# A hybrid decoder step: the scan's buffers in three pools, its skip connection at the group's end, attention spread over 15 blocks

## The chip, the core and the metric

The kernel runs on one core of one Trainium2 chip. A core has five engines that work side by side: TensorE (PE, matrix products; its weight loads are listed as PEld), VectorE (DVE), ScalarE (ACT), GpSimd (POOL) and SyncE (SP, which here only issues transfers). Sixteen DMA engines move data between DRAM and the on-chip memory SBUF. PE writes its results to PSUM, from where DVE and ACT fetch them. The metric is the device time of one execution in microseconds (us); lower is better.

## What is computed

One layer of a decoder, for a prompt of 1024 tokens and eight sample sequences of one token each, all in float32. Three branches read the same normalised input through one input projection, and their results are weighted by gates, added, projected, and followed by a gated feed-forward part. Cut to what matters here:

```
sc_b, sc_c, sc_x, z, xbc, dt_raw, q, gates = split(xn @ w_in)
y_a = (sc_b * conv3(sc_c * sc_x)) @ w_sc_out
xs, bm, cm = split(silu(conv4(xbc) + bias));  dt = softplus(dt_raw + dt_bias)
# scan over chunks of 128 tokens; 4 groups of 8 heads x 64, state 128
y_diag[i] = sum_j (c_i . b_j) * exp(acum_i - acum_j) * dt_j * x_j      (j <= i, same chunk)
y_off[i]  = exp(acum_i) * (c_i . state)
state     = chunk_decay * state + sum_j b_j * decay_j * dt_j * x_j
y_ssd = (y_diag + y_off + ssm_d * xs) * silu(z)
y_b = group_rmsnorm(y_ssd) @ w_ssm_out
y_c = softmax(q @ mem_k.T / 16) @ mem_v @ w_attn_o                      (256 memory tokens, 4 heads)
x += (g_A*y_a + g_B*y_b + g_C*y_c) @ w_merge_o;  x += swiglu(rmsnorm(x));  rmsnorm(x)
```

The term `ssm_d * xs` is called the skip below. The eight sample tokens take the same path with a state of their own; in the kernel they are columns 1024 to 1031 of tiles that are 1032 wide.

## The kernel before

Activations are kept transposed: 128 features on the partitions, 1032 tokens along the row. A float32 product is made of three products of rounded operands (high by high, high by low, low by high). One output block of 128 features is 8 input tiles x 3 products x 3 column thirds of 344, that is 72 matmuls, in `gemm` (the matmuls have line L203). Its weights come from DRAM and are split into a high and a low half by ACT and DVE (L152, L153).

The stretch in question runs as follows. First come the last gate products (`gate_pair`, L775 to L779 write their outputs to `gt_d`). Then 20 blocks of the list `fillers` and of the first output product (eight q blocks `ps_q`, four gate blocks `ps_g`, and the eight blocks `wo00` to `wo07`) run while the scan is worked off in pieces. Then attention is worked off in pieces while the second and third output products run (`wo10` to `wo17`, `wo20` to `wo27`). Then the attention output product `wo30` to `wo37` and the merge follow.

The mixing is done by a queue `pend` of small functions. `gemm` calls `tick()` several times among its matmuls, and each tick runs one function of the queue. `pace` holds how many ticks a block gets and the fraction carried over. This gives the order in the program. A scheduler then sets the order of each engine's instructions, with program order as priority, by its own estimate of when operands are ready; on the chip each engine keeps that order.

The scan, `ssd_pieces`, goes through four groups of eight chunks each, and a chunk is made in three pieces. `first` transposes b and x, makes the masked product `cbm`, multiplies it into the decay matrix `r` and makes `xdt` and `xdd`. `second` makes the state's part `po` and the chunk's part `py` (L941), adds them in `yt` (L937, L946) and adds the skip into x, one operation for each of four feature tiles (L950). `third` updates the state `s`. The decay matrix starts as a broadcast load of `ac_d` into `r` (L882), and ACT makes it ready (`prep`, L888, L889). `s_skip` (L990) does the skip of the eight sample columns. `final` writes out the state. Then `z_pieces` multiplies by silu(z) (L1039) and sums squares (L1047), and `group_norm` makes the sums on PE (`psny`, L1060), spreads the result, scales and stores to `yb_d` (L1084, L1087).

SBUF is divided into pools that open and close like a stack on either side. The scan's tiles are all in one pool, `ssd`, on the right side. It is opened after the pool of the operand forms (`xfx`, 24768 bytes a partition at the outer end) and that of the gate and convolution outputs (`pxa`, next to it) have closed, and lies over parts of both. A group of five shared buffers (`ev`, each 1036 wide) serves most short-lived full-width tiles, and each is taken again once it is free.

Attention ends with the sample's outputs: `s_out` for each of eight sequences, four pieces that write out convolution states (`conv_state`), and `s_back`, which transposes the sample outputs (`psob`, L1509) and stores them to `at_d` (L1511). `out_ahead` and `out_in` load `at_d` (L1301) and split it into the eight inputs `b00` to `b07` of `wo30` (L162, L163).

Of the kernel before, what the change touches and what calls it, by code (L numbers as in the profile page):

```python
# [9 lines left out]
F32 = mybir.dt.float32  # L10
F32R = mybir.dt.float32r
AF = mybir.ActivationFunctionType
ALU = mybir.AluOpType
# [4 lines left out]
P = 128  # L18
D = 1024
T = 1024  # L20
NS = 8
TT = T + NS
# [4 lines left out]
KD = D // P  # L27
EPS = 1e-6
LAG = 3
GROUPS = 4  # L30
HEADS = 32
HPG = 8
# [9 lines left out]
def tile_kernel(ctx: ExitStack, tc, a, o):  # L42
    nc = tc.nc
    V, S, G, PE, SY = nc.vector, nc.scalar, nc.gpsimd, nc.tensor, nc.sync
# [4 lines left out]
    def bc(ap, shape):  # L49
        return ap.to_broadcast(shape)  # L50
# [13 lines left out]
    def sm_ps(name):  # L64
        return psm.tile([P, 512], F32, tag="sm", name=name)
# [4 lines left out]
    def act_tile(part, name, dt=F32R, shape=(P, TT)):  # L70
        return ap_.tile(list(shape), dt, tag=part, name=name)
# [84 lines left out]
    def ev_tile(name, shape=(P, TT + 4), dt=F32):  # L156
        return ev.tile(list(shape), dt, tag="ev", name=name)
# [8 lines left out]
    pend = deque()  # L166
# [12 lines left out]
    pace = [3, 0.0]  # L179
# [209 lines left out]

    ph1 = ExitStack()  # L390
    cn = ph1.enter_context(tc.tile_pool(name="cn", bufs=1))
    h_sc = cn.tile([P, 8, 16], F32, tag="h_sc", name="h_sc")
    h_xc = cn.tile([P, 24, 24], F32, tag="h_xc", name="h_xc")
    xn = [(act_tile("ah", f"xnh{k}"), act_tile("al", f"xnl{k}")) for k in range(KD)]
    xw = [act_tile(("ah", "al")[k % 2], f"xw{k}", F32) for k in range(KD)]
    ps_dt, ps_b0 = mm_ps("ps_dt"), mm_ps("ps_B0")
# [1 line left out]
    with tc.tile_pool(name="p0", bufs=1) as p0:  # L398
# [12 lines left out]
        at = 0  # L411
        for key, src, n in (
# [11 lines left out]
            r = flat_src.rearrange("(r c) -> r c", c=P)  # L424
# [76 lines left out]
        for g3 in range(3):  # L501
            c, n_all = span(g3)
# [17 lines left out]
    for src, dst, nr, nt in (  # L520
# [4 lines left out]
        for q0 in range(0, nt, per):  # L525
            t = ev_tile(f"hist{nr}_{q0}", (nr, per * P))
# [10 lines left out]
    dtT = cn.tile([P, 9, HEADS], F32, tag="dtT", name="dtT")  # L537
    decst = cn.tile([P, NCK, HEADS], F32, tag="decst", name="decst")
    cdec = cn.tile([P, NCK, HEADS], F32, tag="cdec", name="cdec")
    dts = cn.tile([P, 16, NS], F32, tag="dts", name="dts")  # L540
    es = cn.tile([P, 16, NS], F32, tag="es", name="es")
    dpar = cn.tile([P, 16], F32, tag="dpar", name="dpar")
    ys = cn.tile([P, 16, NS], F32, tag="ys", name="ys")
    bcs = cn.tile([P, GROUPS, NS, 2], F32, tag="bcs", name="bcs")

    dt_stack = ExitStack()
    pd_ = dt_stack.enter_context(tc.tile_pool(name="pdt", bufs=1))
# [240 lines left out]
    ssd = ExitStack()  # L788
    pool = {}

    def b3(t, n):
        return t.rearrange("p (a b) -> p a b", a=n)

    def sp_tile(shape, tag, name, bufs=2):
        return pool["ssd"].tile(shape, F32, tag=tag, bufs=bufs, name=name)


    def bc_rows():
# [67 lines left out]
        pair()  # L866
        assert not pend

    def ssd_pieces(g, xg, bcg):
        hs = slice(g * HPG, (g + 1) * HPG)  # L870
        h0 = g * HPG
        state = {}
# [4 lines left out]

        def load(c):
            nm = f"{g}_{c}"
            r = sp_tile([P, HPG, P], "r", "r" + nm, 3)  # L880
            live[c] = r
            SY.dma_start(r, ac_d[g, c].unsqueeze(0).to_broadcast([P, HPG, P]))  # L882

# [7 lines left out]
        def load_ea(c):  # L891
            ea = None
            if c > 0:
                ea = sp_tile([P, 4, P], "ea", f"ea{g}_{c}")
                for k in range(2):
                    SY.dma_start(ea[k * 64 : (k + 1) * 64], ea_d[g, c, 4 * k : 4 * k + 4].unsqueeze(0).to_broadcast([64, 4, P]))
            return ea
# [27 lines left out]
        def second(c):  # L925
            nm = f"{g}_{c}"
            cs = slice(c * P, (c + 1) * P)
            r, ea, xdt, xdd, bT = live[c]
            yt = sp_tile([P, 4, P], "yt", "yt" + nm, 1)
            if c > 0:  # L930
                po = sm_ps("po" + nm)
                for t in range(4):
                    PE.matmul(  # L933
                        po[:, t * P : (t + 1) * P], state["s"][:, t * P : (t + 1) * P], bcg[1][:, cs],
                        start=True, stop=True,
                    )
                V.tensor_tensor(yt, b3(po, 4), ea, op=ALU.mult)  # L937
            py = sm_ps("py" + nm)
            for h in range(HPG):
                hp = (h % 2) * 64  # L940
                PE.matmul(  # L941
                    py[hp : hp + 64, (h // 2) * P : (h // 2 + 1) * P],
                    xdt[:, h * 64 : (h + 1) * 64], r[:, (h % 2) * 4 + h // 2, :], start=True, stop=True,
                )
            if c > 0:
                V.tensor_tensor(yt, b3(py, 4), yt, op=ALU.add)  # L946
            else:
                S.copy(yt, b3(py, 4))
            for t in range(4):
                V.scalar_tensor_tensor(  # L950
                    xg[t][:, cs], xg[t][:, cs], dpar[:, g * 4 + t : g * 4 + t + 1], yt[:, t, :],
                    op0=ALU.mult, op1=ALU.add,
                )

        def third(c):
            nm = f"{g}_{c}"
            r, ea, xdt, xdd, bT = live.pop(c)
            pss = sm_ps("pss" + nm)
            PE.matmul(pss, bT, xdd, start=True, stop=True)  # L959
            if c == 0:  # L960
                s_new = sp_tile([P, 512], "s", "s" + nm)
                ins = V.tensor_copy(s_new, pss)
            else:
                s_new = state["next"]
                ins = V.tensor_tensor(s_new, pss, s_new, op=ALU.add)  # L965
            state["s"] = s_new
            return ins.ins

        def decay(c):

            s_new = sp_tile([P, 512], "s", f"s{g}_{c}")
            G.tensor_tensor(  # L972
                b3(s_new, HPG), b3(state["s"], HPG), bc(cdec[:, c, hs].unsqueeze(2), [P, HPG, 64]),
                op=ALU.mult,
            )
            state["next"] = s_new

        def final():
            ps = sm_ps(f"psf{g}")
            for t in range(4):  # L980
                PE.transpose(ps[:, t * P : (t + 1) * P], state["s"][:, t * P : (t + 1) * P], ident)
            sf = sp_tile([P, 4, P], "yt", f"sf{g}", 1)
            S.copy(sf, b3(ps, 4))
            SY.dma_start(
                o["p_ssm"][0, 0, hs].rearrange("h p n -> (h p) n").rearrange("(t q) n -> q t n", q=P), sf
            )

        def s_skip():
            for t in range(4):
                V.scalar_tensor_tensor(  # L990
                    xg[t][:, T:TT], xg[t][:, T:TT], dpar[:, g * 4 + t : g * 4 + t + 1], ys[:, g * 4 + t, :],
                    op0=ALU.mult, op1=ALU.add,
                )

        def head():
            load(0)
# [34 lines left out]
    def z_load(g, t, hold):  # L1031
        zs = act_tile(("ah", "al")[t % 2], f"zs{g}{t}", F32)
        SY.dma_start(zs, zs_d[g * 4 + t])
        hold[t] = zs

    def z_pieces(g, xg, hold):
        def piece(t):
            zs = hold.pop(t)
            V.tensor_mul(xg[t], xg[t], zs)  # L1039
            if t == 0:  # L1040
                hold["q"] = ev_tile(f"sqa{g}")
            sqa = hold["q"]
            if t == 0:
                S.activation(sqa[:, :TT], xg[t], AF.Square)
            else:
# [236 lines left out]
    gate_pair(18, plain)  # L1282
    st_stack.close()
    pa_stack.close()
    pmm[0] = mm_stack.enter_context(tc.tile_pool(name="pmm1", bufs=2, space=PSUM))


    pool["ssd"] = ssd.enter_context(tc.tile_pool(name="ssd", bufs=2, side="right"))
    fillers = deque()
    for i in range(8):  # L1290
        fillers.extend(q_step(i))
# [61 lines left out]
    outs = deque()  # L1353
# [8 lines left out]
        )  # L1362
    for g in range(GROUPS):
        xg, bcg, hold = groups[g]
        pieces = ssd_pieces(g, xg, bcg)
        if g > 0:
            pend.extend([lambda g=g: load_group(g), None])
        pend.extend(pieces[:-3])
        pend.append(lambda g=g, hold=hold: [z_load(g, t, hold) for t in range(2)])
        pend.extend(pieces[-3:])  # L1370
        pend.extend(z_pieces(g, xg, hold) + [None] + group_norm(g, xg, hold))
    pace[0] = len(pend) / (len(fillers) + KD)
    while fillers or pend:
        if len(fillers) == 1:
            out_ahead(sc_d)
# [24 lines left out]
    at = att_stack.enter_context(tc.tile_pool(name="att", bufs=2))  # L1400
    if True:
# [170 lines left out]
        pieces = [[(kv_in, 0)], [(kv_in, 1), (a_load, 0)], [], []]  # L1572
# [23 lines left out]
        pend.extend(pieces)  # L1596
        pend.extend(states)
        pend.extend([None, s_back])
        pace[0] = 5
        while pend:  # L1600
            run_next(outs)
        pace[0] = 3
        att_stack.close()
        ph2 = ctx.enter_context(tc.tile_pool(name="ph2", bufs=1))
        assert not pend
# [82 lines left out]
    for half in range(2):  # L1688
        sq = ev_tile(f"sq{half}")
        for m in range(KD):  # L1690
# [16 lines left out]
            t = x2[m][:, HS[half]]  # L1707
# [237 lines left out]
```

## Time and profile before

| | before |
|---|---|
| median of 3 runs | 2502.28 us (2502.19 to 2504.86) |
| profiled execution | 2503.04 us, span of its trace 2501.3 us |
| matmuls | 18714 |
| busy: PE, DVE, ACT, POOL | 2461.6, 1519.3, 1047.0, 135.3 us |
| scan with its 20 blocks | about 966 to 1333 us |
| attention with its 14 blocks | about 1333 to 1566 us |
| DMA moved | 392.08 MB, mean 157 GB/s |

A row of the profile gives line, engine, operation, the tiles written and read, their shapes and the count, then busy time, mean duration in ns, and the idle time ahead of the instructions with what ended it. "issue" means that nothing the profile shows was waited for. In a row of the timeline the first number is the start in us from the beginning of the span and the second the time taken.

### The profile page before, as it was taken

To read this page: it belongs to the slowest core of one execution; us is meant where nothing else is said; L and a number is where in the kernel's file an instruction comes from. 1 tells how busy PE (TensorE), PEld (TensorE's weight loads), DVE (VectorE), ACT (ScalarE), POOL (GpSimd) and SP (SyncE) were. 2 spreads that over 40 slices of the span, in tenths; PEclk is the share of its full clock that TensorE was granted. 3 is DMA by queue.
4 is the path that set the end of the run, shared out by engine and by line. 5 is a ranking of instruction groups with operands and counts; after the bars stand their busy time and mean duration, and the time that the engine had idled before them with its cause. 6 is when DMAs were issued, how large, how long until landed. Compare 5 with 4: busy or idle time off the path is not lost.

```text
span 2501.3 us, 44971 instructions
## 1 busy us (share of the span) xinstructions
PE 2461.6 (98%) x18714; PEld 2399.9 (96%) x18714; DVE 1519.3 (61%) x2590; ACT 1047.0 (42%) x1688; POOL 135.3 (5%) x163
## 2 busy tenths in 40 slices
PE   7999999999999999999999999999999999999998
PEld 6999999999999998999989998999999999999998
DVE  6754586777677773766866662655775545453325
ACT  6554455454545534556545441223433333341212
POOL 0300000000000000321120000000000000000000
PEclk9999999999999999999999999999999999999999
DMA  6344434344344455668867686945442222282211
GB/s 202 110 150 154 128 104 143 110 140 126 99 136 136 127 160 190 192 211 266 276 199 277 218 303 218 327 144 178 140 151 95 85 68 85 86 274 89 68 34 69
DMA packets 348331, 392.08 MB, mean 157 GB/s; under 512 B 15334, under 2 KB 285782, under 8 KB 348119
## 3 DMA queue, kind: packets, MB, share of 16 engines
q1 hardware_dynamic: 327678, 331.50, 42.1%
q10 hardware_dynamic: 20449, 57.71, 6.1%
q8 instruction: 147, 2.41, 0.4%
q14 instruction: 57, 0.47, 0.1%
HBM read 280.40 MB, written 108.98 MB: 156 GB/s over the span
## 4 chain that ended last, share of the span: by engine, by line
PE 92%; DVE 2%; DMA 2%; ACT 2%; issue 1%; SPq 0%; ACTq 0%; DVEq 0%; POOL 0%
PE po L203 14%; PE pd L203 9%; PE ps_q L203 4%; PE pm L1701 4%; PE py L941 1%; PE pss L959 1%; PE ps_g L203 1%; PE po L933 1%; PE ps_z L203 1%; PE u20m L248 1%; PE u6m L248 1%; PE g20m L248 1%; PE u18m L248 1%; PE g18m L248 1%; PE u16m L248 1%
## 5 line engine op out<-in xcount | busy, mean ns | idle before, releaser
L1843 DVE TENSOR_TENSOR x<-pd,x 128x1032 f32<-128x1032 f32 x24 | 29.6, 1231 | 131.2 <-PE pd L203 131.2
L888 ACT ACTIVATE r<-r,acum 128x128 f32<-128x128 f32 x256 | 78.8, 391 | 5.3 <-DMA r<-ac_d 4.9
L659 DVE SCALAR_TENSOR_TENSOR ax<-u,prm,ax 128x1024 f32<-128x1024 f32 x44 | 56.3, 1280 | 0.1
L920 POOL TENSOR_TENSOR xdd<-xdt,decst 128x512 f32<-128x512 f32 x32 | 38.0, 1189 | 296.5 <-DVE xdt L916 296.5
L829 ACT ACTIVATE st<-st,es 128x128 f32<-128x128 f32 x128 | 41.9, 394 | 22.4 <-DMA st<-in_state_ssm_dram 20.5
L914 DVE TENSOR_TENSOR r<-r,cbm 128x1024 f32<-128x1024 f32 x32 | 39.0, 1218 | 9.5 <-ACT r L889 9.2
L1348 DVE TENSOR_TENSOR yr<-po,yr 128x1032 f32<-128x1032 f32 x8 | 9.9, 1232 | 53.8 <-PE po L203 53.8
L913 ACT COPY bT<-bp 128x128 f32<-128x128 f32 x32 | 8.5, 265 | 79.9 <-DVE cbm L911 79.9
L831 DVE SCALAR_TENSOR_TENSOR st<-sr,dts,st 128x128 f32<-128x128 f32 x128 | 40.2, 346 | 0.4
L941 PE MATMUL py<-r,xdt 128*64 128x128 f32 x512 | 35.9, 284 | 4.4 <-issue 4.4
L937 DVE TENSOR_TENSOR yt<-po,ea 128x512 f32<-128x512 f32 x28 | 19.3, 689 | 32.5 <-PE po L933 29.7
L941 PEld LDWEIGHTS py<-r,xdt 128*64 128x64 f32 x512 | 28.1, 139 | 8.7 <-issue 5.3
L950 DVE SCALAR_TENSOR_TENSOR x<-x,dpar,yt 128x128 f32<-128x128 f32 x128 | 36.2, 345 | 0.2
L835 DVE SCALAR_TENSOR_TENSOR sr<-st,sr 128x128 f32<-128x128 f32 x128 | 35.4, 286 | 1.1
L972 POOL TENSOR_TENSOR s<-s,cdec 128x512 f32<-128x512 f32 x28 | 35.1, 1253 | 0.5 <-DVE s L965 0.4
L889 ACT ACTIVATE r<-r 128x1024 f32<-128x1024 f32 x32 | 33.9, 1060 | 0.6
L959 PE MATMUL pss<-xdd,bT 128*128 128x512 f32 x64 | 33.5, 605 | 0.0
L1708 DVE TENSOR_TENSOR x<-pm,xT 128x516 f32<-128x516 f32 x16 | 11.1, 696 | 36.4 <-PE pm L1701 36.3
L933 PE MATMUL po<-bc,s 128*128 128x128 f32 x224 | 29.5, 275 | 0.0
L933 PEld LDWEIGHTS po<-bc,s 128*128 128x128 f32 x224 | 28.4, 191 | 0.0
L1630 DVE TENSOR_TENSOR gt<-po,gt 128x1032 f32<-128x1032 f32 x8 | 9.9, 1232 | 30.6 <-PE po L203 28.8
L662 DVE SCALAR_TENSOR_TENSOR ax<-u,prm,ax 128x1032 f32<-128x1032 f32 x22 | 28.3, 1286 | 0.0
(9105 smaller groups left out, 8947.7 us busy)
## 6 DMA issues: line engine op xcount, KB each, us to landing
r<-ac_d SPq DMA_DIRECT2D x32, 512.0 KB
gt<-gt_d SPq DMA_DIRECT2D x24, 516.0 KB
xs_d<-ax ACTq DMA_DIRECT2D x22, 516.0 KB
hr<-h_d SPq DMA_DIRECT2D x22, 516.0 KB
gt_d<-G ACTq DMA_DIRECT2D x20, 516.0 KB
x<-xs_d SPq DMA_DIRECT2D x16, 516.0 KB
zs<-zs_d SPq DMA_DIRECT2D x16, 516.0 KB
yb_d<-x SPq DMA_DIRECT2D x16, 516.0 KB
```

The source lines that it names most:

```text
L203: PE.matmul(ps[:, n, :CW], wt[:, ks], x[:, n * CW : (n + 1) * CW], start=(k == 0 and i == 0), stop=(k == nk - 1 and i == 2),)
L248: PE.matmul(ps[:, n, :HC], wt[:, ks], x[:, n * HC : (n + 1) * HC], start=(start and kt == 0 and i == 0), stop=(kt == 3 and i == 2), skip_g ...
L659: V.scalar_tensor_tensor(acc[:, :T], u[:, j : j + T], w[j], acc[:, :T], op0=ALU.mult, op1=ALU.add)
L829: S.activation(st[:, i], st[:, i], AF.Copy, scale=es[:, g * 4 + i, b : b + 1])
L831: V.scalar_tensor_tensor(st[:, i], rb, dts[:, g * 4 + i, b : b + 1], st[:, i], op0=ALU.mult, op1=ALU.add)
L888: S.activation(r[:, j, :], r[:, j, :], AF.Relu, scale=-1.0, bias=acum[:, c, h : h + 1])
L914: V.tensor_tensor(r, r, bc(cbm.unsqueeze(1), [P, HPG, P]), op=ALU.mult)
L920: G.tensor_tensor(b3(xdd, HPG), b3(xdt, HPG), bc(decst[:, c, hs].unsqueeze(2), [P, HPG, 64]), op=ALU.mult)
L933: PE.matmul(po[:, t * P : (t + 1) * P], state["s"][:, t * P : (t + 1) * P], bcg[1][:, cs], start=True, stop=True,)
L941: PE.matmul(py[hp : hp + 64, (h // 2) * P : (h // 2 + 1) * P], xdt[:, h * 64 : (h + 1) * 64], r[:, (h % 2) * 4 + h // 2, :], start=True, s ...
L959: PE.matmul(pss, bT, xdd, start=True, stop=True)
L1701: PE.matmul(ps[:, n, :HC], wt[:, ks], x[:, half * HT + n * HC : half * HT + (n + 1) * HC], start=(k == 0 and i == 0), stop=(k == KD - 1 an ...
```

## The change

Four things are changed.

- The tiles that only the phase ahead of the scan needs (`h_sc`, `h_xc`, `dts`, `es`, `bcs`) move into a pool `ch` of their own, which is closed ahead of the scan. The scan's single pool becomes three, opened in the order `ssr` (the three `r` buffers), `ssd` (`cbm`, `bT`, `xdt`, `xdd`) and `ssy` (`ea`, `s` and the new `y`).
- The outputs of a group's chunks are written to one tile `y` of 4 x 1032, one buffer, in place of `yt` of 4 x 128. The skip is no longer added chunk by chunk; it is one full-width operation for each feature tile at the head of each piece in `z_pieces`. The sample columns are copied into `y` (four copies in place of sixteen small operations). The state that `final` writes out takes an `ev` buffer in place of `yt`.
- The pace in the scan is set anew with its carried fraction at zero and a millionth added.
- The pace in attention, 5 pieces a block, becomes the number of pieces divided by the blocks that are left but one (15).

```diff
-    h_sc = cn.tile([P, 8, 16], F32, tag="h_sc", name="h_sc")
-    h_xc = cn.tile([P, 24, 24], F32, tag="h_xc", name="h_xc")
+    ch_stack = ExitStack()
+    ch = ch_stack.enter_context(tc.tile_pool(name="ch", bufs=1))
+    h_sc = ch.tile([P, 8, 16], F32, tag="h_sc", name="h_sc")
+    h_xc = ch.tile([P, 24, 24], F32, tag="h_xc", name="h_xc")
...
-    def sp_tile(shape, tag, name, bufs=2):
-        return pool["ssd"].tile(shape, F32, tag=tag, bufs=bufs, name=name)
+    def sp_tile(shape, tag, name, bufs=2, at="ssd"):
+        return pool[at].tile(shape, F32, tag=tag, bufs=bufs, name=name)
...
-            r = sp_tile([P, HPG, P], "r", "r" + nm, 3)
+            r = sp_tile([P, HPG, P], "r", "r" + nm, 3, "ssr")
...
-                ea = sp_tile([P, 4, P], "ea", f"ea{g}_{c}")
+                ea = sp_tile([P, 4, P], "ea", f"ea{g}_{c}", at="ssy")
...
-            yt = sp_tile([P, 4, P], "yt", "yt" + nm, 1)
+            if c == 0:
+                hold["y"] = sp_tile([P, 4, TT], "y", f"y{g}", 1, "ssy")
+            yt = hold["y"][:, :, cs]
...
-            for t in range(4):
-                V.scalar_tensor_tensor(
-                    xg[t][:, cs], xg[t][:, cs], dpar[:, g * 4 + t : g * 4 + t + 1], yt[:, t, :],
-                    op0=ALU.mult, op1=ALU.add,
-                )
...
-            sf = sp_tile([P, 4, P], "yt", f"sf{g}", 1)
+            sf = ev_tile(f"sf{g}", (P, 4, P))
...
         def s_skip():
-            for t in range(4):
-                V.scalar_tensor_tensor(
-                    xg[t][:, T:TT], xg[t][:, T:TT], dpar[:, g * 4 + t : g * 4 + t + 1], ys[:, g * 4 + t, :],
-                    op0=ALU.mult, op1=ALU.add,
-                )
+            V.tensor_copy(hold["y"][:, :, T:TT], ys[:, g * 4 : g * 4 + 4, :])
...
             zs = hold.pop(t)
+            V.scalar_tensor_tensor(
+                xg[t], xg[t], dpar[:, g * 4 + t : g * 4 + t + 1], hold["y"][:, t, :], op0=ALU.mult, op1=ALU.add
+            )
             V.tensor_mul(xg[t], xg[t], zs)
...
     pa_stack.close()
+    ch_stack.close()
...
-    pool["ssd"] = ssd.enter_context(tc.tile_pool(name="ssd", bufs=2, side="right"))
+    for name in ("ssr", "ssd", "ssy"):
+        pool[name] = ssd.enter_context(tc.tile_pool(name=name, bufs=2, side="right"))
...
-    pace[0] = len(pend) / (len(fillers) + KD)
+    pace[:] = len(pend) / (len(fillers) + KD) + 1e-6, 0.0
...
-        pace[0] = 5
+        pace[:] = len(pend) / (len(outs) - 1) + 1e-6, 0.0
         while pend:
             run_next(outs)
-        pace[0] = 3
+        pace[:] = 3, 0.0
```

The diff leaves out that `dts`, `es` and `bcs` also move from `cn` to `ch`, that the two tiles of `s` move to `ssy`, and that `ssd_pieces` is handed `hold`.

More of the change, by code (lines that the diff above doesn't have):

```diff
@@ L539, in tile_kernel @@
     cdec = cn.tile([P, NCK, HEADS], F32, tag="cdec", name="cdec")
-    dts = cn.tile([P, 16, NS], F32, tag="dts", name="dts")
-    es = cn.tile([P, 16, NS], F32, tag="es", name="es")
+    dts = ch.tile([P, 16, NS], F32, tag="dts", name="dts")
+    es = ch.tile([P, 16, NS], F32, tag="es", name="es")
     dpar = cn.tile([P, 16], F32, tag="dpar", name="dpar")
     ys = cn.tile([P, 16, NS], F32, tag="ys", name="ys")
-    bcs = cn.tile([P, GROUPS, NS, 2], F32, tag="bcs", name="bcs")
+    bcs = ch.tile([P, GROUPS, NS, 2], F32, tag="bcs", name="bcs")
     dt_stack = ExitStack()
@@ L867, in with_steps, with ssd_pieces @@
         assert not pend
-    def ssd_pieces(g, xg, bcg):
+    def ssd_pieces(g, xg, bcg, hold):
         hs = slice(g * HPG, (g + 1) * HPG)
@@ L960, in third @@
             if c == 0:
-                s_new = sp_tile([P, 512], "s", "s" + nm)
+                s_new = sp_tile([P, 512], "s", "s" + nm, at="ssy")
                 ins = V.tensor_copy(s_new, pss)
@@ L969, in decay @@
         def decay(c):
-            s_new = sp_tile([P, 512], "s", f"s{g}_{c}")
+            s_new = sp_tile([P, 512], "s", f"s{g}_{c}", at="ssy")
             G.tensor_tensor(
@@ L1364, in tile_kernel @@
         xg, bcg, hold = groups[g]
-        pieces = ssd_pieces(g, xg, bcg)
+        pieces = ssd_pieces(g, xg, bcg, hold)
         if g > 0:
```

## The prediction

> **What bounds the kernel now.** I read the page first (span, part 1, the chain), then stretches of the span, the waits, and the order of instructions at three seams: the scan's start, a group's end, the hand-over from attention to the third output product.
>
> ```profile
> span 2501.3 us, 44971 instructions
> PE 2461.6 (98%) x18714; PEld 2399.9 (96%) x18714; DVE 1519.3 (61%) x2590; ACT 1047.0 (42%) x1688; POOL 135.3 (5%) x163
> PE 92%; DVE 2%; DMA 2%; ACT 2%; issue 1%; SPq 0%; ACTq 0%; DVEq 0%; POOL 0%
> ```
>
> TensorE is busy 98% of the span and carries 92% of the chain. The change adds and removes no matmul and no transpose, so only PE's idle time and its clock can move: 2501.3 − 2461.6 = 39.7 us of idle over the whole program. Stretches of it, where the columns are the window's length, busy time of PE, PEld, DVE, ACT, POOL, the granted clock, DMA share and GB/s:
>
> ```profile
> core 0: us, PE busy (x) PEld busy (x) DVE busy (x) ACT busy (x) POOL busy (x), PEclk, DMA share, GB/s
> 965.30:973.80 8.50, 8.50 (x57) 8.34 (x56) 1.23 (x1) 1.54 (x2) 0.00 (x0) 1.00 1.00 314
> 980.90:985.40 4.50, 0.06 (x3) 0.05 (x2) 1.23 (x1) 4.47 (x11) 0.00 (x0) 0.77 0.19 44
> 985.40:990.10 4.70, 4.70 (x27) 4.37 (x28) 1.77 (x4) 4.54 (x12) 0.19 (x1) 0.50 0.49 159
> 1043.00:1056.40 13.40, 13.40 (x86) 12.90 (x84) 11.75 (x14) 6.31 (x7) 3.90 (x1) 1.00 0.93 292
> 1326.00:1333.00 7.00, 7.00 (x42) 7.00 (x41) 2.08 (x2) 1.05 (x1) 0.00 (x0) 0.76 0.79 272
> 1330.00:1360.00 30.00, 30.00 (x195) 29.25 (x195) 17.97 (x21) 14.07 (x19) 0.00 (x0) 0.98 0.81 287
> 1345.00:1566.00 221.00, 218.73 (x1460) 201.98 (x1458) 114.69 (x295) 80.90 (x170) 0.00 (x0) 1.00 0.73 249
> 1566.00:1680.00 114.00, 114.00 (x727) 113.50 (x728) 62.96 (x55) 27.79 (x27) 0.00 (x0) 1.00 0.75 252
> ```
>
> The one long gap in the stretch that the change touches stands at 980.9 to 985.4, and behind it the clock is at half for 4.70 us of work.
>
> **1. Three pools at the scan's start (a gain).** Why PE waits there:
>
> ```profile
> DVE cbm L911 <- DMA gt_d<-G: 5.5, 1, 5.5
> PE py L941 <- issue: 4.4, 1, 4.4
> ...
> 965.65 0.97 SPq L1033 DMA_DIRECT2D zs<-zs_d  x2
> 973.88 1.27 SPq L882 DMA_DIRECT2D r<-ac_d  x3
> ...
> 966.29 0.33 ACTq L779 DMA_DIRECT2D gt_d<-G  x1
> 978.91 2.74 ACT L888 ACTIVATE r<-r,acum 128x128 f32<-128x128 f32 x9 [4.39 <-DMA r<-ac_d]
> ...
> 985.38 0.91 PE L941 MATMUL py<-r,xdt 128*64 128x128 f32 x6 [4.44 <-issue]
> ...
> 977.64 0.50 PEld L203 LDWEIGHTS ps_q<-xnh,wq1h 128*128 128x128 f32 x3
> ```
>
> The gate's last store, issued at 966.29, holds the whole scan: cbm and the first r load start together at 973.9, when it lands. The one pool lies over the gate's output buffers, so it must wait for them. The pool for r (3 × 4096 B = 12288 B a partition) and the one for cbm, bT, xdt, xdd (10240 B) together fit under the 24768 B of the operand forms (six 128x2x516 buffers), which the last matmuls free; only the third pool (ea, y, s) lies over the gate's buffers. So r can be issued at about 965.65, where the zs loads went, 8.2 us earlier. It took 978.91 − 973.88 = 5.0 us to arrive. With the store and weight loads still in flight (DMA share 1.00 in 965.3 to 973.8) I bound the arrival by 970.7 (5.0 us again) and 973.8 (8.2 us, all that this traffic lasted), and take 973.0, near the busy end because the DMA engines are full. From arrival to py it was 985.38 − 978.91 = 6.47 us of ACT and DVE: py is ready at 977.2 to 980.3, say 979.5. PE reaches py at 980.9 in its old place, but the scheduler may pull it to where the code has it, the head of the second block, 977.64: a rest of 0 to 2.7 us. I take 1.5. Saved: 4.44 − 1.5 = **2.9 us** (1.7 to 4.4). The half clock over 4.70 us of work costs 2.35 us; I count **2.35 us** saved, bounds 0 and 2.35, for the row at 1326 to 1333 has clock 0.76 with PE busy throughout, so a stall is not the only thing that brings it.
>
> A rule to weigh: the Trainium skill, "TensorE: Matmul & The Clock Gate", sections "What's actually happening" and "Why this matters for your kernels", has the clock halve after an idle window of about 3.4 us and keep its rate over gaps under some 3 us. By it the rest of 1.5 us surely keeps the clock and the 2.35 us are all saved; by the 0.76 row they may not be, and the sum would be 2.35 us worse.
>
> On SP, the ea loads now wait for the store where r waited; behind them stand zs and weight loads whose readers come much later, which I cost at nothing; if that cover is gone it is a block's weights late, bounded by the same 8.2 us.
>
> **2. The skip at the group's end (no path change expected).**
>
> ```profile
> L950 DVE SCALAR_TENSOR_TENSOR x<-x,dpar,yt 128x128 f32<-128x128 f32 x128 | 36.2, 345 | 0.2
> L990 DVE SCALAR_TENSOR_TENSOR x<-x,dpar,ys 128x8 f32<-128x8 f32 x12 | 2.7, 222 | 10.6 <-DMA x<-xs_d 10.6
> L1084 DVE SCALAR_TENSOR_TENSOR x<-x,prm,sqa 128x1032 f32<-128x1032 f32 x12 | 14.7, 1288 | 3.8 <-ACT sqa L1080 3.8
> ...
> 1043.82 1.14 DVE L950 SCALAR_TENSOR_TENSOR x<-x,dpar,yt 128x128 f32<-128x128 f32 x4
> ```
>
> 128 small operations (36.2 us) become 16 full-width ones at 1.288 us (the same operation and shape at L1084): 20.6 us. Sixteen tail operations at 0.222 us, 3.6 us, become four copies, under 0.9 us. DVE does 36.2 + 3.6 − 20.6 − 0.9 = 18.3 us less. That buys nothing on PE directly. But at a group's end, between the last chunk and the norm's sums, the 1.14 us of four small ones go and about 4 × 1.2 = 4.8 us come in: 3.7 us more in a chain on DVE, once a group. Cover: in 1043 to 1056.4 PE is busy 13.40 of 13.40 us with product matmuls, and the next group starts when its data come. I take 0; if the cover is gone, 4 × 3.7 = 14.8 us. The single y buffer of a group is free once the fourth full-width operation has read it, well before the next group's first chunk writes: 0. The state's output copy now takes one of the five shared ev buffers until its store has landed; at the last group these also feed the next product's inputs. PE is busy 30.00 of 30.00 us in 1330 to 1360, so 0, with 0 to 2 us as bounds.
>
> **3. Attention over 15 blocks (a loss).** The pieces number 43 + 4 + 16 + 4 + 2 = 69. At 5 a block they end in the 14th (wo25), at 4.6 in the 15th (wo26): the last piece, s_back, comes one block later, and the product that needs it, wo30, stays. The chain there:
>
> ```profile
> 1556.26 7.68 DMA out_s_xconv_dram<-cs
> 1564.06 1.87 DMA osr<-os_d
> ...
> 1566.92 0.37 SPq L1511 DMA_DIRECT2D at_d<-o_s  x1
> 1573.64 0.32 SPq L1301 DMA_DIRECT2D in<-at_d  x1
> ...
> 1579.23 1.06 ACT L162 CAST b00h<-in 128x1032 fp32r<-128x1032 f32 x1 [2.80 <-DMA in<-at_d]
> 1552.65 0.72 PE L203 MATMUL po<-b00h,wo25h 128*128 128x344 f32 x3
> 1564.17 0.64 PE L203 MATMUL po<-b00h,wo26h 128*128 128x344 f32 x3
> 1588.66 0.63 PE L203 MATMUL po<-b00h,wo30h 128*128 128x344 f32 x3
> ```
>
> A block is 1564.17 − 1552.65 = 11.52 us. Shifted by that, the first at_d load goes at 1585.2, and its cast starts 5.59 us later as before (1579.23 − 1573.64), at 1590.8, done 1591.8. PE wants it at 1588.66: 3.1 us. Within the block s_back sits at k = 6 instead of 4 and its buffers one or two k later, 1.4 us each (11.52/8): up to 2.8 us more. Against that, osr waited 7.68 us for a buffer held by a conv-state store; if it finds another, the chain is up to 6 us earlier and hidden. Bounds 0 and 5.9, and with half clock behind the stall 2.35 more; I take **4.0 us**. Once the first input is there the rest follow at about PE's rate, for the two first products share each of them. Inside attention fewer pieces a block can change PE's 221.00 − 218.73 = 2.27 us of idle by that much either way; I take 0. In the scan the pace stays 158 pieces over 20 blocks.
>
> **Sum.** −2.9 − 2.35 + 0 + 4.0 = −1.3 us against the profiled execution's 2503.04 us (span 2501.3), which lies 0.76 us above the median of 2502.28: about **2501.0 us**.
>
> **Rivals.**
> Faster: s_back finds a buffer early or PE's order covers it, so part 3 costs 0 to 1 us. Time 2502.28 − 5.3 + 0.5 = 2497.5, down to 2495.5 with the stall gone whole. For it: the 7.68 us wait for a buffer is an accident of the order. Against: the pieces are on PE at their place in the code, and the last place is now wo26.
> Slower: the hand-over at wo30. The late at_d input stalls PE for 5.9 us, the clock halves behind it (2.35 us), and the inputs, which arrived just as PE took them, stay late by another 2 to 4 us; with a part 1 of 3 us that gives 2502.28 − 3 + 8.25 + 3 = 2510.5. PE begins to wait once at_d's store lands later than 1588.66 − 6.65 = 1582.0 on the old scale (5.59 + 1.06 us from load to the end of the cast), and the whole is slower than before once it lands past 1582.0 + 5.25 = 1587.3.
> The change does not do what it says: the first stall and its half clock stay, because py is moved up by as much as r comes earlier. With part 3 at 4.0 us and half clock behind that wait too: 2502.28 + 4.0 + 2.35 = 2508.6. For it: the order was off by 4.44 us once already. Against: py can hardly go ahead of 977.64.
> Cover gone at the groups' ends: 2501 + 14.8 = 2516, unlikely, as each group's PE order is full of products.
>
> **How the numbers follow.** The likeliest, both effects near cancelling, 0.42: 2501.0, its own range 2498 to 2505. Faster rival 0.28. Slower hand-over 0.18, first stall kept 0.08, cover gone 0.04. From 2493.5 (the faster rival with everything saved and 2 us of attention's idle too) to 2510.5 about 0.85 is held. A measurement of this kernel tells about 0.2% (5 us) from no change: faster 0.28, same 0.42, slower 0.30.
>
> **What would show it.** Part 1: the first r load near 965.7 and py's wait under 2.7 us, clock 1.00 behind. Part 2: sixteen 1.29 us operations just ahead of the zs products, no new PE wait at the norm's sums. Part 3: s_back's transposes near wo26's end, the first at_d load near 1585, a PE wait of some 4 us ahead of wo30. I am wrong if PE shows no wait there, or if the first r is still late.

## The result and the profile after

The changed kernel takes 2509.6 us (median of 6 runs, 2507.88 to 2515.59); the kernel before, run on the same chip, 2502.24 us (2500.27 to 2504.86). The ratio is 1.0029, with a 95% interval from 1.0019 to 1.0039: it became 0.3% slower. The forecast was 2501.0 us with 2510.5 as upper end.

The profiled execution took 2507.88 us. The first lines of its page (span, busy times, engines of the chain):

```profile
span 2506.2 us, 44839 instructions
PE 2461.6 (98%) x18714; PEld 2397.3 (96%) x18714; DVE 1504.3 (60%) x2466; ACT 1048.8 (42%) x1688; POOL 127.5 (5%) x163
PE 85%; DMA 6%; DVE 4%; ACT 3%; issue 1%; SPq 0%; ACTq 0%; POOL 0%; DVEq 0%
```

PE has the same matmuls and the same busy time. DVE lost 15.0 us of work, and the time still grew by 4.9 us of span. What grew is the part of the chain that is not PE: 15% now, 8% before. So the question is where PE waits. The starts of the first matmuls of `wq0` (the scan's first block), `wo10` (attention's first block) and `wo32` (behind the hand-over) divide both traces into four stretches:

| stretch, us | before | after | difference |
|---|---|---|---|
| up to wq0 | 966.31 | 968.23 | +1.92 |
| scan, wq0 to wo10 | 367.18 | 357.33 | −9.85 |
| attention and hand-over, wo10 to wo32 | 278.26 | 292.20 | +13.94 |
| the rest | 889.56 | 888.39 | −1.17 |

In the first and the last stretch the two kernels do the same work; these stretches vary by such amounts among the runs below. The scan gained more than forecast, and attention lost far more.

**The scan's start.** Rows of the timeline of the changed kernel (start, time taken, engine, line, operation, and in brackets the idle time ahead of it and its releaser):

```profile
966.12 1.31 SPq L884 DMA_DIRECT2D r<-ac_d  x3
...
971.33 2.46 ACT L890 ACTIVATE r<-r,acum 128x128 f32<-128x128 f32 x8 [2.83 <-DMA r<-ac_d]
...
976.38 3.05 SPq L898 DMA_DIRECT2D ea<-ea_d  x4
...
979.80 1.09 PE L945 MATMUL py<-r,xdt 128*64 128x128 f32 x16
```

The r load goes at 966.12, where it went at 973.88 before; ACT starts on it 5.2 us later, and `py` runs at 979.80 without a wait (4.44 us before). The loads of ea took over the wait for the gate's store, at 976.38, and nobody waits for them.

**Attention.** The wait of PE that stands first in its list (what PE wanted, what ended the wait; us in total, times, longest), and stretches of attention in the columns that the prediction explained:

```profile
PE psp L1549 <- ACT pr L1455: 3.9, 1, 3.9
```

```profile
1345.00:1580.00 235.00, 226.08 (x1488) 208.18 (x1487) 112.07 (x293) 82.82 (x170) 0.00 (x0) 0.99 0.71 237
1473.00:1478.40 5.40, 1.52 (x11) 1.24 (x10) 5.05 (x6) 4.22 (x8) 0.00 (x0) 1.00 0.94 331
1478.50:1482.00 3.50, 3.50 (x16) 3.50 (x14) 3.46 (x18) 1.70 (x6) 0.00 (x0) 0.53 0.55 224
1580.00:1620.00 40.00, 38.62 (x242) 36.97 (x242) 26.37 (x23) 13.18 (x13) 0.00 (x0) 1.00 0.94 312
```

PE is idle 235.00 − 226.08 = 8.92 us in attention's stretch; before it was 2.27 us in a like one. The largest piece stands at 1473, where the second product (wo17) hands over to the third (wo20), with half clock behind it (0.53). I call this place the seam. What ACT does there, one row of DVE, and the waiting PE instruction:

```profile
1460.26 1.05 ACT L162 CAST b00h<-in 128x1032 fp32r<-128x1032 f32 x1 [7.06 <-DMA in<-yb_d]
...
1470.03 0.47 ACT L1455 ACTIVATE pr<-psa,mx 128x256 f32<-128x256 f32 x1
1471.67 1.06 ACT L162 CAST b05h<-in 128x1032 fp32r<-128x1032 f32 x1 [0.63 <-DMA in<-yb_d]
...
1475.09 1.05 ACT L162 CAST b07h<-in 128x1032 fp32r<-128x1032 f32 x1 [1.18 <-DMA in<-yb_d]
1475.66 0.16 DVE L1453 TENSOR_SCALAR mx<-mx 128x2 f32<-128x2 f32 x1
1476.99 0.47 ACT L1455 ACTIVATE pr<-psa,mx 128x256 f32<-128x256 f32 x1
...
1478.06 0.87 PE L1549 MATMUL psp<-ident,pr 128*128 128x128 f32 x4 [3.88 <-ACT pr L1455]
```

The casts b00h to b07h make the third product's eight inputs out of loads from `yb_d` that arrive one by one. ACT keeps its order, so the exponentials of head 3's softmax (L1455), which now lie among these casts, come behind loads that they do not need. DVE does the same to the maxima that the exponentials need: the last step of one (L1453, at 1475.66) stands behind the subtraction `b06l`, which started at 1474.52 and took 1.22 us. PE's `psp` waits for the exponential.

The loads are late as well. Their rows on SP:

```profile
1450.26 1.68 SPq L1302 DMA_DIRECT2D in<-yb_d  x3
...
1463.07 8.79 SPq L1302 DMA_DIRECT2D in<-yb_d  x5
```

The first goes 2.2 us ahead of wo17's first matmul (1452.41); with 14 blocks (e1 below) it goes 11.9 us ahead (1442.41 and 1454.32), and in the kernel before 12.0 us. In SP's list of waits, one load waits 9.4 us for a store of attention's outputs to `at_d`, after which a shared buffer is free.

**The hand-over to wo30**, at the end of attention:

```profile
1586.40 4.14 SPq L1302 DMA_DIRECT2D in<-at_d  x3
...
1591.45 1.05 ACT L162 CAST b00h<-in 128x1032 fp32r<-128x1032 f32 x1 [1.45 <-DMA in<-at_d]
...
1592.56 0.74 PE L203 MATMUL po<-b00h,wo30h 128*128 128x344 f32 x3
```

The first `at_d` load goes at 1586.40, and PE takes its cast almost as it ends, then waits in pieces: 40.00 − 38.62 = 1.38 us of idle between 1580 and 1620, where before there was none.

### The profile page after: what moved, and what is told of

Read it like the earlier page. It is cut to its first block, busy times and chain, and to the rows that moved or that the text cites. A ratio compares the mean times of both kernels' runs of the same rounds, so it can differ in the third digit from the quotient of the medians.

```text
span 2506.2 us, 44839 instructions
## 1 busy us (share of the span) xinstructions
PE 2461.6 (98%) x18714; PEld 2397.3 (96%) x18714; DVE 1504.3 (60%) x2466; ACT 1048.8 (42%) x1688; POOL 127.5 (5%) x163
## 4 chain that ended last, share of the span: by engine, by line
PE 85%; DMA 6%; DVE 4%; ACT 3%; issue 1%; SPq 0%; ACTq 0%; POOL 0%; DVEq 0%
PE po L203 11%; PE pd L203 9%; PE pm L1702 4%; PE ps_q L203 3%; PE ps_g L203 1%; PE py L945 1%; PE pss L958 1%; PE po L937 1%; PE ps_z L203 1%; PE C5m L248 1%; PE Z10m L248 1%; PE G18m L248 1%; PE Z6m L248 1%; PE B6m L248 1%; PE X14m L248 1%
## 5 line engine op out<-in xcount | busy, mean ns | idle before, releaser
L941 DVE TENSOR_TENSOR y<-po,ea 128x512 f32<-128x512 f32 x28 | 19.3, 690 | 36.5 <-PE po L937 36.5
L918 DVE TENSOR_TENSOR xdt<-xp,dtT 128x512 f32<-128x512 f32 x32 | 21.9, 685 | 19.0 <-PE xp L911 18.9
L658 ACT ACTIVATE ax<-u,prm 128x1024 f32<-128x1024 f32 x22 | 27.4, 1247 | 2.7 <-DVE u L344 1.5
```

## The experiments

The theory was that attention over 15 blocks makes the loss and the scan's parts a gain; the rival, that the scan's new order makes it. The kernel before ran beside each group of experiments; its median was 2503.56, 2503.5, 2502.34 and 2503.06 us (2502.24 beside the changed kernel), so medians of different groups can differ by 1.3 us for that reason alone. "Attention" below is the stretch from wo10 to wo32 of the profiled execution, "scan" that from wq0 to wo10.

**Each part by itself.** First the changed kernel with the old pace:

```
-        pace[:] = len(pend) / (len(outs) - 1) + 1e-6, 0.0
+        pace[:] = 5, 0.0
```

> The changed kernel with attention's pace put back to 5 pieces a block (14 blocks). Theory A (the loss is in attention over 15 blocks, the scan's part gains): wo10 starts about 8 us earlier than before, as in the changed kernel, and nothing is given back, so 2494 to 2497 us. Rival B (the loss is in the scan's part, by the order it leaves behind): 2507 to 2510 us, as the changed kernel.

Measured: 2498.84 us (2495.61 to 2501.49), ratio 0.9983 [0.9974, 0.9992]; scan 356.38 us, attention 280.66 us. One line, the pace, decides between faster and slower. It came out a little above the theory's window, and far from the rival's. At the seam only the last of the eight casts, b07h, waits for its load, and head 3's last exponentials (from 1464.48) are ahead of all casts from b03h on:

```profile
1442.41 16.19 SPq L1302 DMA_DIRECT2D in<-yb_d  x5
...
1464.48 0.48 ACT L1455 ACTIVATE pr<-psa,mx 128x256 f32<-128x256 f32 x1
...
1465.64 1.09 ACT L162 CAST b03h<-in 128x1032 fp32r<-128x1032 f32 x1
...
1474.03 1.05 ACT L162 CAST b07h<-in 128x1032 fp32r<-128x1032 f32 x1 [1.48 <-DMA in<-yb_d]
```

Then the kernel before with the new pace alone:

```
-        pace[0] = 5
+        pace[:] = len(pend) / (len(outs) - 1) + 1e-6, 0.0
```

> The kernel before with attention over 15 blocks alone. Theory A: the scores of head 3 fall on the seam between wo17 and wo20, where ACT waits for the yb_d loads, and s_back comes a block later: 2510 to 2516 us, with waits of PE at psp near the seam and about 2 us at wo30. Rival B: 2501 to 2504 us.

Measured: 2512.28 us, ratio 1.0038 [1.0025, 1.005], as the theory expected; scan 367.11 us (unchanged), attention 289.72 us, 11.46 us more than before. The two longest of PE's waits in attention stand where the theory had them:

```profile
PE psp L1548 <- ACT pr L1454: 4.0, 1, 4.0
PE po L203 <- ACT b00h L162: 2.2, 1, 2.2
```

The rival falls.

Then the three pools alone (`r` in `ssr`; `ea`, `yt`, `s` in `ssy`; the skip as before, 14 blocks):

```
-    pool["ssd"] = ssd.enter_context(tc.tile_pool(name="ssd", bufs=2, side="right"))
+    for name in ("ssr", "ssd", "ssy"):
+        pool[name] = ssd.enter_context(tc.tile_pool(name=name, bufs=2, side="right"))
```

> The kernel before with the scan's one pool cut into three, yt and the skip chunk by chunk as before, 14 blocks. If the first gap at py (4.44 us) and the half clock behind it are what the pools remove: py's wait under 2.7 us, clock 1.00 in 983 to 990, 2495.5 to 2499.5 us. If the gap stays because the order moves py up as well: 2501 to 2503 us.

Measured: 2497.82 us, ratio 0.9978 [0.9969, 0.9987]: the gain was there, 5.7 us. The 4.4 us wait of py and the half clock behind it are gone; no period at half clock begins between 62.9 us and 2493.2 us.

Last the skip at the group's end alone (one pool, 14 blocks):

```
-    for name in ("ssr", "ssd", "ssy"):
-        pool[name] = ssd.enter_context(tc.tile_pool(name=name, bufs=2, side="right"))
+    pool["ssd"] = ssd.enter_context(tc.tile_pool(name="ssd", bufs=2, side="right"))
+    pool["ssr"] = pool["ssy"] = pool["ssd"]
```

> The changed scan (one y tile a group, skip at the group's end) in one pool, 14 blocks. My sum has this part at 0: the first gap of about 4.4 us stays, 2501 to 2504 us. If the full-width skips shorten PE's path: 2497 to 2500. Rival B (they lengthen the groups' ends): 2507 us or more.

Measured: 2505.68 us, ratio 1.0008 [0.9999, 1.0016], 2.1 us above and not told from no change; it lies above the window of my sum (2501 to 2504) and below the rival's (2507). PE's waits from the scan's start into attention:

```profile
PE py L945 <- issue: 4.2, 1, 4.2
PE pskT L1422 <- DVE kTl L1425: 1.7, 1, 1.7
```

The first stall stays, as it should, and a wait for `kTl` at attention's start is new; it appears in every kernel with the skip at the group's end.

**Two places in attention.** Three theories for the 15 blocks: the seam and the later s_back both cost (A1), s_back alone (A2), the seam alone (A3). The pace is changed behind the softmax of the samples, the 44th of the 69 pieces, once upward with the slow start (e5) and once downward with the fast start (e6):

```
-        pieces += [s_softmax, lambda: s_values(0), s_probs, None]
+        def late():
+            s_softmax()
+            pace[:] = 6, 0.0        # e5; in e6: 4, 0.0, and 5 in the place of 69/15 at the start
+        pieces += [late, lambda: s_values(0), s_probs, None]
```

> The changed kernel with its 15-block pace up to the softmax of the samples (piece 44) and six pieces a block behind it, so that s_back stands in wo25 again, as in 14 blocks; the seam wo17/wo20 is left as it is. Theory A1 (the loss in attention has two places, 5 us at the seam and 2 to 3 us in front of wo30 through the later s_back): the seam's wait of about 4 us ahead of psp stays, the waits in wo30 and wo31 go, and the time is 2506.5 to 2508. Theory A2 (s_back alone makes the loss, as the prediction had it): 2498 to 2501. Theory A3 (the seam alone): 2509 to 2511.

> The changed kernel with five pieces a block up to the softmax of the samples and four behind it, so that head 3's scores lie in wo17 as in 14 blocks and s_back in wo26 as in 15. Theory A1: no wait over 1 us ahead of psp near the seam, 2 to 3 us of waits around wo30, 2500.5 to 2503. Theory A2 (s_back alone): 2507 to 2511. Theory A3 (the seam alone): 2497.5 to 2500.

| | early pieces, 4.6 a block | early pieces, 5 a block |
|---|---|---|
| late pieces, slower | after: 2509.6 us, attention 292.20 | e6: 2500.38 us, attention 280.76 |
| late pieces, faster | e5: 2506.59 us, attention 289.73 | e1: 2498.84 us, attention 280.66 |

With the slow start attention takes 289.73 − 280.66 = 9.07 us longer even where the end is fast (7.75 us in the medians), and e5 lies in A1's window. A2 is out. The seam's wait stands in e5's list as in the changed kernel's, 3.9 us of psp for ACT's `pr`. The stretches at and behind it:

```profile
1476.00:1481.30 5.30, 1.39 (x10) 1.11 (x10) 4.90 (x8) 4.07 (x8) 0.00 (x0) 1.00 0.97 349
1481.30:1485.00 3.70, 3.70 (x17) 3.70 (x16) 3.35 (x16) 1.63 (x7) 0.00 (x0) 0.54 0.52 188
```

The wait's 3.9 us and half of the 3.4 us at half clock make 5.6 of the 9.07; smaller waits of psp and psa (1.5 and 0.8 us) most of the rest. The slower end costs 292.20 − 289.73 = 2.47 us behind the slow start, and 0.10 us behind the fast one. There s_back's transposes stand 14.7 us ahead of wo30 (1568.26 and 1582.97), against 10.1 us in the changed kernel (1582.45 and 1592.56), so e6 is not the full test of the end that it was meant to be; its time, 2500.38, lies just between the windows of A1 and A3.

**What at the seam?** If two casts emitted ahead of wo20 (b06, b07) hold the exponential, they can be emitted inside wo20's loop instead:

```
-        for k in range(len(acts), KD):
-            ...
-            acts.append(split_act(ahead.popleft()[:, :TT], f"b0{k}"))
+        if src is not ins[2][0]:
+            while len(acts) < KD:
+                more()
+        else:
+            seam.append(lambda k: more() if k > 1 else None)
```

> The changed kernel, 15 blocks, with the last two casts of the third product's inputs (b06, b07) issued inside wo20's loop over k (at k=2 and 3) and not ahead of it. Theory B1 (the exp of head 3 stands behind b06h and b07h on ScalarE, b07h waiting 1.2 us for its load): exp starts about 3 us earlier, the wait of 3.9 us ahead of psp at the seam falls below 1 us, the half clock behind it goes, 2504 to 2506.5. Theory B2 (the loads are late whatever the order, and TensorE would wait for b06 or b07 itself): the wait moves to po<-b06h or b07h, 2508.5 to 2510.5.

Measured: 2509.29 us, ratio 1.0023 [1.0013, 1.0032]; attention 291.14 us. PE's waits near the seam, and from the timeline the row of instructions that ends with the exponential:

```profile
PE psa L1544 <- ACT pr L1464: 2.2, 1, 2.2
PE psp L1558 <- ACT pr L1464: 1.7, 1, 1.7
```

```profile
1473.52 1.05 ACT L162 CAST b05h<-in 128x1032 fp32r<-128x1032 f32 x1 [0.53 <-DMA in<-yb_d]
...
1474.61 1.24 DVE L163 TENSOR_TENSOR b05l<-in,b05h 128x1032 fp32r<-128x1032 f32 x1 [0.54 <-ACT b05h L162]
1475.76 0.68 DVE L1461 TENSOR_REDUCE mx<-psa 128x2 f32<-128x512 f32 x1
...
1476.74 0.47 ACT L1464 ACTIVATE pr<-psa,mx 128x256 f32<-128x256 f32 x1 [2.16 <-DVE mx L1462]
```

Neither theory had it right as a whole. The exponential did move ahead by about 3 us, as B1 expected: it starts 117.7 us behind wo12's first matmul, against 120.8 us in the changed kernel. But PE's wait did not fall below 1 us, because the exponential now waits for the maximum on DVE, and DVE stands in its own order behind the subtraction b05l, which waits for the cast and the load of b05. The wait did not move to b06 or b07 either, though the time lies in B2's window: it split into two, 1.7 and 2.2 us (the second for the next exponential, which waits for its maximum in turn), the half clock went, and the seam gained 1.85 us (wo12 to wo21 took 137.49 us, 139.34 in the changed kernel), of which 0.8 was lost again up to wo32 (122.97 and 122.18 us from wo21 on). So the last two casts are not enough to explain the seam: the subtractions on DVE hold the maxima, as the casts on ACT hold the exponentials.

To take the cause away whole, the third product reads the second product's inputs again, in 15 blocks (e9) and in 14 (e10):

```
     def out_in(src):
+        if src is ins[2][0]:
+            return
         ...
-        if m == KD - 1:
+        if m == KD - 1 and i != 1:
             out_ahead(nxt)
```

> The changed kernel, 15 blocks, whose third product reads the second product's inputs again: the eight loads of yb_d and the eight casts and subtractions b00 to b07 ahead of wo20 are left out, so its output is not the reference's. Theory C1 (these loads and casts, one after another on ScalarE and VectorE with head 3's softmax between them, make the wait at the seam): no wait over 1 us ahead of psp near wo20, no half clock there, and 1.5 to 4 us more than the same kernel in 14 blocks (e10), which is what the later s_back costs. Theory C2 (fewer pieces a block cost by themselves, or head 3 meets something else there): 8 to 11 us more than e10, as with the inputs.

> The same without the third product's own inputs (output not the reference's), with five pieces a block (14 blocks). Its loads and casts are not waited for in the kernel with them, so both theories expect 2495.5 to 2499 us, up to 3 us below the 2498.84 with them; it is the measure for e9.

Measured: 2502.85 us (2499.68 to 2507.45) with 15 blocks, 2498.19 us (2495.72 to 2500.49) with 14: 4.7 us apart, where with the inputs it was 10.8 (2509.6 and 2498.84). In the traces attention takes 285.63 and 281.36 us, 4.27 apart against 11.54. Without the inputs the kernel with 14 blocks is as fast as with them (0.65 us), the one with 15 blocks 6.7 us faster. That shows the seam: in the traces its loads, casts and subtractions make 11.54 − 4.27 = 7.27 us of attention's loss. They were left out together, so these two runs do not say how much of it the late loads make and how much the order on ACT and DVE. What is left in e9, in its list of PE's waits (leaving out the one for kTl) and in the stretches at wo30:

```profile
PE po L203 <- ACT b00h L162: 1.7, 1, 1.7
PE psp L1551 <- DVE pTl L1559: 1.5, 2, 0.8
```

```profile
1581.00:1585.50 4.50, 2.78 (x16) 2.21 (x16) 3.89 (x4) 2.28 (x3) 0.00 (x0) 1.00 0.91 319
1585.60:1589.00 3.40, 3.40 (x14) 3.40 (x13) 3.12 (x3) 1.33 (x2) 0.00 (x0) 0.50 1.08 352
```

The 1.7 us ahead of wo30 and half of 3.4 us at half clock are the later s_back, 3.4 us. The difference was a little above the 4 us that C1 allowed; the psp waits of 1.5 us fill that. These come with 4.6 pieces a block, with the seam's inputs (1.5 us in e5) and without.

**Other block counts.** `pace = len(pend) / 13`:

> The changed kernel with attention over 13 blocks (pace 5.31). If what counts is that head 3's scores are through before the seam (theory A1), it behaves as with 14 blocks: no wait over 1.5 us near wo20, 2497.5 to 2501. If fewer blocks crowd ScalarE and the loads (the rival, by which 15 blocks would have helped elsewhere): 2503 to 2508.

Measured: 2504.87 us, ratio 1.0004 [0.9995, 1.0013], attention 289.20 us. The theory that head 3 need only be early enough missed by 4 us, and the time lies in the rival's window:

```profile
PE pso L1493 <- DMA vc<-in_cache_mem_v_dram: 2.8, 1, 2.8
PE psv L1567 <- ACT ot L1570: 2.4, 1, 2.4
```

There is no psp wait over 0.3 us, as expected, although the loads of `yb_d` are late here too: the first goes 1.7 us ahead of wo17 (1462.88 and 1464.62), and the casts wait for them, behind head 3's last exponentials:

```profile
1466.09 0.47 ACT L1455 ACTIVATE pr<-psa,mx 128x256 f32<-128x256 f32 x1 [0.49 <-DVE mx L1453]
...
1474.62 1.05 ACT L162 CAST b03h<-in 128x1032 fp32r<-128x1032 f32 x1 [1.14 <-DMA in<-yb_d]
```

Loads as late as this did not make PE wait where head 3's softmax stood ahead of the casts. But at 13 blocks the sample outputs overtake their loads and `psv` meets ACT, and each of these waits is followed by half clock (from 1447.9 and 1502.5 us, 3.4 us each). Of 13, 14 and 15 blocks, 14 is the best, for different reasons on either side.

**Which pool?** The kernel before with a pool for `r` alone, the rest together:

```
-            r = sp_tile([P, HPG, P], "r", "r" + nm, 3)
+            r = sp_tile([P, HPG, P], "r", "r" + nm, 3, "ssr")
+    pool["ssr"] = ssd.enter_context(tc.tile_pool(name="ssr", bufs=2, side="right"))
     pool["ssd"] = ssd.enter_context(tc.tile_pool(name="ssd", bufs=2, side="right"))
```

> The kernel before with only the scan's r tiles in a pool of their own, ahead of the rest. If the r tiles' place, behind what the Strassen stage leaves last, makes the first stall (the prediction's part 1), the wait of 4.4 us ahead of py goes and the time is 2496.5 to 2499.5, as with three pools. If it is the others' place (ea, yt, s): the wait stays, 2501 to 2503.

Measured: 2499.53 us, ratio 0.9987 [0.9978, 0.9996]; scan 361.11 us (three pools 360.39), at the upper edge of the first window. In the trace py waits 0.96 us and the next xp 1.4 us:

```profile
980.78 1.09 PE L941 MATMUL py<-r,xdt 128*64 128x128 f32 x16 [0.96 <-issue]
...
985.24 0.66 PE L909 MATMUL xp<-ident,x 128*128 128x128 f32 x4 [1.40 <-ACT yt L948]
```

The place of r makes the long stall. With a pool for cbm, bT, xdt and xdd apart from ea, yt and s (e3) py does not wait and xp waits 0.3 us; the intervals of the two kernels overlap.

**A version that beats both.** The three pools alone (2497.82 us) and the changed kernel in 14 blocks (2498.84 us) are both faster than either kernel and not told apart. The second still has the wait for kTl. On DVE kTl stands behind wo14's subtraction there, and ahead of it with the pools alone; so the subtraction was put behind it:

```
+        with tc.issue_after(held[name]) if name in held else nullcontext():   # held["wo14"]: the first kTl
             in_turn("lo", V.tensor_sub(lo, raw, f32(hi)))
```

> The changed kernel in 14 blocks, with VectorE's subtraction for wo14 issued behind the first half's kTl and not ahead of it, as the kernel with three pools alone has it. Theory D1 (pskT waits 1.7 us at attention's start because kTl stands behind wo14's subtraction on VectorE): the wait falls below 0.5 us and the time by 1.2 to 2.5 us against the 2498.84 without it, 2496.3 to 2497.7, below the kernel before and the changed kernel. Theory D2 (kTl is late for its own input, the cast kTh on ScalarE): the wait stays, 2498 to 2500.

Measured: 2499.53 us, ratio 0.9984 [0.9975, 0.9993], no faster than without. From its timeline:

```profile
1352.20 1.05 ACT L152 CAST wo14h<-wo14r 128x1024 fp32r<-128x1024 f32 x1 [2.33 <-PE po L203]
1353.15 1.07 ACT L1424 CAST kTh<-pskT 128x512 fp32r<-128x512 f32 x2
...
1354.51 1.25 PE L1422 MATMUL pskT<-ident,kk 128*128 128x128 f32 x8 [1.00 <-DVE kTl L1425]
```

The wait fell from 1.65 to 1.00 us only, for on ACT the cast kTh stands behind wo14's cast in the same way, and the stretch from wo10 to wo12 takes 30.64 us as without the edit (30.67). D2 is the nearer one. The three pools alone have the lowest median of the kernels run, 0.22% below the kernel before [0.13%, 0.31%].

## Why the prediction was wrong

The forecast had the parts at −5.25, 0 and +4.0 us. Run one at a time they measured −5.7, +2.1 and +8.7 us against their 2503.56 us. That makes +5.1 us, where all together measured +7.4 us (2509.6 against 2502.24), so single medians do not add up to better than about 2 us. Most of the error is in the third part.

**Part 1** was right in mechanism and in size (5.7 us). One step was too cautious: I had r arrive at 973.0, since the DMA engines were full, within bounds of 970.7 to 973.8. In the changed kernel ACT started on it at 971.33, which is 969.4 on the old scale (wq0 starts 1.92 us later), ahead of both bounds. So py had no rest of 1.5 us to wait. The half clock went as taken, and the one at 1328 went too, which I had left in place.

**Part 2**: the operations are as counted, sixteen at 1.288 us:

```profile
L1034 DVE SCALAR_TENSOR_TENSOR x<-x,dpar,y 128x1032 f32<-128x1032 f32 x16 | 20.1, 1288 | 0.1
```

DVE lost 15.0 us where I had 18.3. "That buys nothing on PE directly" and "I take 0" for the longer chain hide two effects of opposite sign. Between the kernels with three pools, without and with the skip at the end, the scan shrank from 360.39 to 356.38 us, and the first two blocks of attention grew from 27.88 to 30.67: there lie 1.65 us of waiting for kTl, in place of 1.08 us for `yr`, and the last group's 18 norm sums (`psny`, 2.06 us), which came ahead of wo10 before. The net of the two stretches is near 0 in the traces (−1.2 us) and in the medians (+1.0); with one pool it was +2.1 us, inside its measurement's width. Why the scan shrank by more than what moved out of it wasn't separated.

**Part 3** failed. The step of the prediction that failed is: "Inside attention fewer pieces a block can change PE's 221.00 − 218.73 = 2.27 us of idle by that much either way; I take 0." It measured 9.07 us in the traces and 7.75 us in the medians (e5 against e1), most of it at the seam. The error is in the bound. The idle time of the old order limits what a new order can win, but not what it can lose: a loss comes from waits that the old trace does not have. The row of casts at the seam was in the old trace, its last one waiting for its load:

```profile
1476.18 1.10 ACT L162 CAST b06h<-in 128x1032 fp32r<-128x1032 f32 x1
...
1481.06 1.06 ACT L162 CAST b07h<-in 128x1032 fp32r<-128x1032 f32 x1 [1.37 <-DMA in<-yb_d]
```

PE did not feel it because nothing that PE wanted soon stood behind it. The waits of the other casts for their loads are new. To see the loss ahead I had to lay the 69 pieces out at 4.6 a block: head 3's scores and their transposes are pieces 34 to 40, counted from 0. With 15 blocks wo17 has 32 to 35 and wo20 has 36 to 40, with the casts among them; with 14, wo17 has 35 to 39, and all but the last were through ahead of wo20.

The s_back term was right in mechanism and near in size: 4.0 us forecast, bounds 0 to 5.9; it measured 2.5 us (e5 to after), and 3.4 us with its half clock where the seam doesn't come first (e9). In the changed kernel the sign that I had named, a PE wait of some 4 us ahead of wo30, was 1.38 us in pieces. The first at_d load, forecast near 1585, went at 1586.40, with wo24 1.60 us later than before.

The rival for "slower", the hand-over at wo30, gave 2510.5 us and so about the right time, by luck and for another reason: what came is mostly the seam, one product earlier.

On the clock, the row after the seam's wait (0.53 in 1478.5 to 1482) is one period at half rate, 1.7 us lost. I had 2.35 us as the price, from a place where two such periods followed each other.

## What to carry to other kernels

A pace is a layout: changing the number of pieces a block moves every piece against every fixed event, so each fixed row of in-order work (casts fed one by one from loads, above all) has to be held against the pieces that will now lie in it. A stretch with little idle time bounds the gain of a new order and says nothing about its loss. And parts of a change should be timed singly: here a part worth 0.2% lay under one that cost 0.4%.

## What was not expected of the hardware

**Half clock comes in periods on a fixed grid.** In the granted clock's record of the kernel before, the periods at half rate ahead of the program's end begin at 61.7, 123.1, 983.3 and 1328.0 us: 18, 270 and 371 times 3.413 us after the first; each is one or two such periods long. In the other traces the starts lie on such a grid too. The Trainium skill, "TensorE: Matmul & The Clock Gate", section "What's actually happening", has a free-running window of 3413 ns, and these traces agree.

**How much idle time costs a period.** I worked out PE's idle time in the period ahead of each half-rate one from its matmuls: 3.11 us in the changed kernel's seam, 2.59 in e5, 2.42 and 2.26 in e8, and 1.72 in e9 (the row from 1581 to 1585.5 above). In e7 about 3.9 us of waiting at the seam fell mostly into two periods, with 1.50 and 1.77 us of idle, and neither cost a clock:

```profile
1475.00:1483.50 8.50, 4.64 (x33) 4.07 (x32) 6.79 (x21) 4.44 (x12) 0.00 (x0) 1.00 0.83 272
```

So about half a period of idle decided in these rows (1.72 us were enough once, 1.77 us were not), with the phase of the grid, not the length of the wait. The Trainium skill, "TensorE: Matmul & The Clock Gate", section "Why this matters for your kernels", names gaps above some 3 us; by these rows a wait of 1.7 us can be enough and one of 3.9 us in two parts harmless. A half-rate period right behind another came with less: the second one in e2, from 991.4, followed 0.8 us of idle.

**Half clock without any idle time.** Before, PE was busy all of the period ahead of 1328.0 and the next was granted half:

```profile
1324.60:1328.00 3.40, 3.40 (x28) 3.37 (x28) 2.25 (x2) 0.47 (x1) 0.00 (x0) 1.00 1.01 406
1328.00:1331.40 3.40, 3.40 (x13) 3.40 (x13) 1.23 (x1) 0.58 (x1) 0.00 (x0) 0.50 1.01 311
```

Such periods also came in e4 (1151.3 and 1335.7) and e8 (1144.1), and between 122 and 124 us in seven of the fourteen kernels, the kernel before and the changed one among them. What brings them stays open.
